# Banded attention: three more gate steps between the first scores, and VectorE scales the probabilities of the first 128 tokens

## The chip, the cores and the metric

One Trainium2 core runs the whole kernel; seven more stay unused. The metric is the device time of one execution in microseconds. The engines are TensorE (PE), VectorE (DVE), ScalarE (ACT), GpSimd (POOL) and SyncE (SP), which here only issues DMAs. Times in the traces count from the start of the profiled span.

## The reference, cut to what matters

One decoder layer over 1024 tokens of width 1024. A combined projection feeds three token mixers (a convolution, a state-space scan "SSD", banded attention) and three sigmoid gates that weigh their results; memory cross-attention and an MLP follow. The change lies in the banded attention:

```python
def swa_branch(q, k, v, q_g, k_g, sinks, rel_bias, band_dist):   # 16 heads of 64, 4 kv heads
    q, k = rms_norm(q, q_g), rms_norm(k, k_g)
    # 8 blocks of 128 queries; each sees its own 128 keys and the 128 before
    logits = einsum("bnqgrd,bnkgd->bngrqk", qb, kb) * 64 ** -0.5 + rel_bias
    logits = where(mask, logits, NEG_INF)          # 0 <= distance < 128; block 0 has no keys before it
    m = maximum(max(logits, -1), sink)
    pexp = exp(logits - m)
    probs = pexp / (sum(pexp, -1) + exp(sink - m))
    return einsum("bngrqk,bnkgd->bnqgrd", probs, vb)
...
gates = sigmoid((u @ w_in)[..., OFF_GATE:] + gate_bias)          # 24 tiles of 128 channels here
merged = gates[0] * y_a + gates[1] * y_b + gates[2] * y_c
```

## The kernel before, in words

Large products are done as three float32r products of split operands (high x high, high x low, low x high), with 128x128 weights and 512 moving columns. TensorE runs nearly without a break, and its instructions are kept in program order (`pe.on = True`). A planner orders the other engines' instructions; each engine then works its own list in order, and semaphores join them. Work under `tc.high_priority()` (weight loads and splits in `wslot`, the first splits of the merge) is planned ahead of its place in the program. Weights go through three slots: a load on SP's queue (L158), a cast on ScalarE (L162), and for the low half either a negated copy on ScalarE (L165) with an accumulating load on GpSimd's queue (L166) or a subtraction on GpSimd (L168).

The 24 gate tiles fill TensorE's time between the small, dependent matmuls of the scan and the attention. `fillers()` is a stream of steps of 3 matmuls (128x128 by 512): 21 gates of 16 steps each, then `merge_head`, 32 steps that begin the merging stage (the product of the scan's result with `w_b0`, for two output tiles at once). `fill(n)` takes `round(2 * n)` steps of that stream. A gate ends with a tanh on ScalarE (L296) and a store on SP's queue (L297). `merge_head` loads tiles of the scan's result (L308, `yin`), casts each on ScalarE (L267, `oh`) and subtracts on VectorE (L268, `ol`); its first two staging buffers are shared with the gates' tanh tiles.

The attention handles 16 pieces in `order`, eight blocks `n` of 128 tokens with two halves of 8 heads each. `scores(n, half)` is a generator with two groups: 8 matmuls of queries with keys into two PSUM banks (tile `ps_lg`), then 4 VectorE instructions (L1014) that add the bias, write the logits `lg` to SBUF and keep each row's maximum. After the second group VectorE forms the negated maximum (`nm`, L1022) and the sink's term (`es`, L1023), ScalarE the exponentials with their row sums (L1026, 8 of them), VectorE the reciprocals (`rd`, L1032), and one multiply by the reciprocals (L1033) makes probabilities of the whole piece: 128 x 8 x 128 elements in block 0, twice that in the others. `turned` transposes the probabilities on TensorE (`ps_pt`) and copies them to SBUF on ScalarE (`pT`, L1048); `values` multiplies by the values (`ps_o`) and stores the result (L1065). Small PSUM tiles share four banks (pool `pss`).

Ahead of the main loop come the scores of pieces 0 and 1 (block 0, both halves), with filler steps after each group. Pass `i` of the main loop then takes `turned` of piece `i` and `scores` of piece `i + 2` in turn, one filler step after each of the four, and `values` of piece `i - 1`. The passes 14 and 15 have no scores left. Behind the loop the rest of the fillers runs without a break (L1085).

Of the kernel before, what the change touches and what calls it, by code (L numbers as in the profile page):

```python
# [55 lines left out]
def trunk_kernel(tc, w_io):  # L56
    nc = tc.nc
    act, dve, pool = nc.scalar, nc.vector, nc.gpsimd
    ctx = ExitStack()
    with ctx:  # L60
# [29 lines left out]
        def step():  # L90

            steps_done[0] += 1
            owed[0] += pace[0]
            if owed[0] >= 1:
                owed[0] -= 1
                next(taps[0], 0)
            for i, (due, fn) in enumerate(side):
                if due <= steps_done[0]:
                    side.pop(i)
                    fn()  # L100
                    break
# [181 lines left out]
        with ExitStack() as s1:  # L283
# [43 lines left out]
            def fill(n):  # L327

                for _ in range(round(2 * n)):
                    if next(gates, 0) is None:  # L330
                        filled[0] += 1
                        if filled[0] % 2 == 0:
                            step()
# [435 lines left out]
            with ExitStack() as sc:  # L769
# [197 lines left out]
                def queries(n):  # L967
                    qn[n] = ap_.tile([P, 8, P], F32, tag="qn", name="qn", bufs=2)
                    nc.sync.dma_start(qn[n], d_q[n])
# [20 lines left out]
                def scores(n, half):  # L990

                    if half == 0 and n:
                        queries(n)
                    k0 = 0 if n else P
                    kn = 256 - k0
                    lg = at.tile([P, 8, 256], F32, tag="lg", name="lg", bufs=3)
                    mx = at.tile([P, 8], F32, tag="mx", name="mx")

                    for p2 in range(2):
                        if p2:  # L1000
                            yield
                        banks = [pss.tile([P, 512], F32, tag="s", name="ps_lg") for j in range(2)]
                        for q in range(2):
                            pr = p2 * 2 + q
                            for j in range(2):
                                kv = slice(j * 64, j * 64 + 64)
                                pe.matmul(
                                    banks[j][:, q * 256:q * 256 + kn], qn[n][kv, half * 4 + pr, :],
                                    ktp[kv, half, n * P + P - kn:n * P + P], start=True, stop=True,
                                )  # L1010
                        for q in range(2):
                            for j in range(2):
                                i = (p2 * 2 + q) * 2 + j
                                dve.tensor_tensor_reduce(  # L1014
                                    lg[:, i, k0:], banks[j][:, q * 256:q * 256 + kn], bias[:, half * 8 + i, k0:], 1.0, NEG,
                                    ALU.add, ALU.max, mx[:, i:i + 1],
                                )
                    nm = at.tile([P, 8], F32, tag="nm", name="nm")
                    es = at.tile([P, 8], F32, tag="es", name="es")
                    rs = at.tile([P, 8], F32, tag="rs", name="rs")  # L1020
                    sk = slice(half * 8, half * 8 + 8)
                    dve.scalar_tensor_tensor(nm, mx, -1.0, nsink[:, sk], ALU.mult, ALU.min)  # L1022
                    dve.tensor_sub(es, nm, nsink[:, sk])  # L1023
                    act.activation(es, es, AF.Exp)
                    for i in range(8):
                        act.activation(  # L1026
                            lg[:, i, k0:], lg[:, i, k0:], AF.Exp, bias=nm[:, i:i + 1],
                            accum_out=rs[:, i:i + 1],
                        )
                    dve.tensor_add(rs, rs, es)  # L1030
                    rd = at.tile([P, 8], F32, tag="rd", name="rd")
                    dve.reciprocal(rd, rs)  # L1032
                    pool.tensor_mul(  # L1033
                        lg[:, :, k0:], lg[:, :, k0:], rd.unsqueeze(2).to_broadcast([P, 8, kn])
                    )
                    lgs.append(lg)
                    yield
# [32 lines left out]
                lgs, pTl = [], []  # L1070
                for o in order[:2]:
                    for _ in scores(*o):
                        fill(1)
                fill(4)
                for i, o in enumerate(order):
                    pieces = [turned(*o, lgs[i]), scores(*order[i + 2]) if i + 2 < len(order) else iter(())]
                    for _ in range(2):
                        for piece in pieces:
                            next(piece, 0)
                            fill(0.5)  # L1080
                    if i:
                        values(*order[i - 1], pTl[i - 1])
# [122 lines left out]
        with ExitStack() as sc:  # L1205
# [67 lines left out]
            def attend(h, qT, outs, first, start):  # L1273
# [64 lines left out]
                for at, fn, args in (  # L1338
                    (0, scores, (0,)), (2, scores, (1,)), (5, turn, (0,)), (6, scores, (2,)), (7, turn, (1,)),
                    (8, scores, (3,)), (10, values, (0, 0)), (11, values, (0, 1)), (12, turn, (2,)), (13, turn, (3,)),  # L1340
                    (15, values, (1, 0)), (16, values, (1, 1)),
                ):
                    after(start + at, lambda fn=fn, args=args: fn(*args))
# [375 lines left out]
def build(nc, packed):  # L1719
    io = {k: nc.dram_tensor(k, v.shape, mybir.dt.from_np(v.dtype), kind="ExternalInput").ap() for k, v in packed.items()}  # L1720
    io["outT"] = nc.dram_tensor("outT", (KT, P, T), F32, kind="ExternalOutput").ap()
    with tile.TileContext(nc) as tc:
        trunk_kernel(tc, io)
# [12 lines left out]
```

## Time and profile before

| | us |
|---|---|
| median of 3 runs (range) | 2715.16 (2714.44 to 2717.03) |
| the profiled execution | 2716.95 |
| its span | 2715.2 |
| TensorE busy | 2681.2 (99%) |
| VectorE, ScalarE, GpSimd busy | 1605.4, 1074.0, 794.6 |
| attention: first and last scores start | 1184.9, 1327.9 |

Rows of the timeline give the start, the length, the engine, the line, the operation, the tiles written and read, the shapes and how many instructions are joined; the bracket holds the idle time before it and what ended it. A row of a stretch gives its length, then the busy time of each engine with its instructions, the granted TensorE clock (1.00 is full), the share of the DMA engines and the bytes moved. Matmul lengths overlap each other, so steps are read from start to start.

### The profile page before, as it was taken

Reading aid. Unit: us, or ns where it says so; the run is one execution under the profiler, and the core shown is the slowest. Engines: PE = TensorE matmul, PEld = TensorE weight load, DVE = VectorE, ACT = ScalarE, POOL = GpSimd, SP = SyncE. Lnnn points to the kernel's source line nnn. Section 1 sums busy time; section 2 is a strip of 40 time slices with the busy share of each in tenths; the row PEclk is TensorE's granted clock in tenths of the full one; section 3 lists DMA queues with packets and bytes.
Section 4 is the critical chain, followed back from the end, with each engine's and each line's share of the span. In section 5 each row is a group of like instructions: output and inputs, shape, how many; then the busy total and the mean of one; then the engine's idle time right before and its main releaser. Section 6 shows DMA issues by size and latency. Waiting matters only on the chain. (4 is left out here: it accounts for less than half of the span.)

```text
span 2715.2 us, 31722 instructions
## 1 busy us (share of the span) xinstructions
PE 2681.2 (99%) x12368; PEld 2164.6 (80%) x12368; DVE 1605.4 (59%) x1887; ACT 1074.0 (40%) x1749; POOL 794.6 (29%) x442
## 2 busy tenths in 40 slices
PE   9999999999999999999999999999998999999999
PEld 7888878888787878775588778888876888888887
DVE  7598878758666776524414773434568886532423
ACT  6533321225666656556612351324423332222221
POOL 2332221200505050414342432321115664422220
PEclk9999999999999999999999999999999999999999
DMA  7642232344555555672444332311123332454642
GB/s 249 204 131 95 96 114 88 122 125 86 148 155 148 142 146 154 179 228 76 140 178 155 117 109 93 101 58 32 59 85 109 147 132 109 179 187 140 207 134 70
DMA packets 119574, 354.79 MB, mean 131 GB/s; under 512 B 12016, under 2 KB 37120, under 8 KB 119040
## 3 DMA queue, kind: packets, MB, share of 16 engines
q1 hardware_dynamic: 112656, 328.12, 35.8%
q0 software_dynamic: 6768, 24.64, 5.4%
q8 instruction: 97, 1.59, 0.2%
q14 instruction: 53, 0.43, 0.1%
HBM read 277.06 MB, written 78.80 MB: 131 GB/s over the span
## 5 line engine op out<-in xcount | busy, mean ns | idle before, releaser
L73 PE MATMUL ps_g<-oh,wh 128*128 128x512 f32 x1872 | 604.3, 403 | 9.1 <-ACT oh L267 3.9
L73 PE MATMUL ps_g<-ol,wh 128*128 128x512 f32 x1872 | 591.8, 394 | 3.0 <-DVE ol L268 2.8
L73 PE MATMUL ps_g<-oh,wl 128*128 128x512 f32 x1872 | 582.1, 391 | 1.5 <-POOL wl L168 1.5
L168 POOL TENSOR_TENSOR wl<-ws,wh 128x1024 fp32r<-128x1024 f32 (+2 forms) x106 | 261.9, 2472 | 714.7 <-ACT wh L162 682.6
L73 PEld LDWEIGHTS ps_g<-ol,wh 128*128 128x128 f32 x1872 | 351.8, 188 | 89.3 <-issue 9.3
L73 PEld LDWEIGHTS ps_g<-oh,wl 128*128 128x128 f32 x1872 | 352.2, 188 | 77.2 <-POOL wl L168 1.9
L73 PEld LDWEIGHTS ps_g<-oh,wh 128*128 128x128 f32 x1872 | 339.0, 189 | 73.0 <-issue 5.5
L362 DVE SCALAR_TENSOR_TENSOR tapy<-hin,cst,tapy 128x1024 f32<-128x1024 f32 x240 | 354.6, 1477 | 32.7 <-ACT tapy L357 26.2
L162 ACT CAST wh<-ws 128x1024 fp32r<-128x1024 f32 (+1 forms) x169 | 176.4, 1044 | 466.9 <-PE ps_g L73 303.1
L73 PE MATMUL ps_up<-blk,st 128*128 128x512 f32 x1344 | 310.0, 393 | 8.8 <-DVE blk L1387 5.7
L73 PEld LDWEIGHTS ps_up<-blk,st 128*128 128x128 f32 x1344 | 254.3, 190 | 63.8 <-DVE blk L1387 6.3
L268 DVE TENSOR_TENSOR ol<-r_in,oh 128x1024 fp32r<-128x1024 f32 x64 | 91.7, 1437 | 222.8 <-ACT oh L267 222.8
L73 PE MATMUL ps_d<-ol,wh 128*128 128x512 f32 x512 | 199.5, 390 | 0.4 <-DVE ol L268 0.2
L73 PE MATMUL ps_d<-oh,wl 128*128 128x512 f32 x512 | 199.2, 389 | 0.0
L73 PE MATMUL ps_d<-oh,wh 128*128 128x512 f32 x512 | 199.2, 389 | 0.0
L73 PE MATMUL ps_tm<-wh,oh 128*128 128x512 f32 x448 | 175.8, 393 | 0.4 <-DVE zth L637 0.4
L73 PE MATMUL ps_tm<-wh,ol 128*128 128x512 f32 x448 | 174.6, 390 | 0.0
L73 PE MATMUL ps_tm<-wl,oh 128*128 128x512 f32 x448 | 174.4, 389 | 0.0
L166 POOL DMA_DIRECT2D wl<-w_ch x45 | 39.1, 868 | 378.6 <-ACT wl L165 378.6
L182 POOL TENSOR_TENSOR wl<-ws,wh 128x1024 fp32r<-128x1024 f32 x28 | 76.3, 2736 | 218.1 <-ACT wh L181 218.0
L267 ACT CAST oh<-r_in 128x1024 fp32r<-128x1024 f32 x64 | 67.2, 1053 | 180.1 <-PE ps_d L73 173.0
L791 DVE SCALAR_TENSOR_TENSOR c4a<-c4v,cst,c4a 128x1023 f32<-128x1023 f32 (+2 forms) x72 | 96.6, 1341 | 59.5 <-ACT c4a L789 48.4
(388 smaller groups left out, 3843.6 us busy)
## 6 DMA issues: line engine op xcount, KB each, us to landing
r_in<-d_r SPq DMA_DIRECT2D x64, 512.0 KB, 3.7
ws<-w_ch SPq DMA_DIRECT2D x63, 512.0 KB, 3.5
wl<-w_ch POOLq DMA_DIRECT2D x45, 512.0 KB, 5.8
csb<-d_cs SPq DMA_DIRECT2D x32, 512.0 KB, 4.0
gth<-d_th SPq DMA_DIRECT2D x32, 512.0 KB, 4.4
ws<-w_up SPq DMA_DIRECT2D x32, 512.0 KB, 3.3
d_r<-r SPq DMA_DIRECT2D x32, 512.0 KB, 2.6
ws<-w_down SPq DMA_DIRECT2D x32, 512.0 KB, 3.3
```

The costliest lines, as they stand in the source:

```text
L73: ins = nc.tensor.matmul(*a, **k)
L162: act.copy(wh[:, a:b], st[:, a:b])
L166: pool.dma_start(wl[:, a:b], src[:, a:b], accum_op=ALU.add)
L168: (low or pool).tensor_sub(wl[:, a:b], st[:, a:b], wh[:, a:b].bitcast(F32))
L182: pool.tensor_sub(wl[:, :, c], s3, wh[:, :, c].bitcast(F32))
L267: act.copy(a, src)
L268: dve.tensor_sub(b, src, a.bitcast(F32))
L362: dve.scalar_tensor_tensor(y, hin[:, j:j + T], w(j), y, ALU.mult, ALU.add)
L791: dve.scalar_tensor_tensor(a[:, s:], v[:, :T - s], C("c4_w", ct * 4 + 3 - s), a[:, s:], ALU.mult, ALU.add)
```

## The change

The multiply by the reciprocals is issued on VectorE for block 0 (two instructions) and on GpSimd for the other blocks as before. The steps of filler after each of the four groups of scores ahead of the main loop become 3 instead of 2; the fourth group is followed by 8 more in both versions. The number of filler steps in all is the same, so four fewer are left for the run behind the loop.

```diff
                     dve.reciprocal(rd, rs)
-                    pool.tensor_mul(
+
+                    (pool if n else dve).tensor_mul(
                         lg[:, :, k0:], lg[:, :, k0:], rd.unsqueeze(2).to_broadcast([P, 8, kn])
                     )
                     lgs.append(lg)
...
                 lgs, pTl = [], []
                 for o in order[:2]:
                     for _ in scores(*o):
-                        fill(1)
+                        fill(1.5)
                 fill(4)
                 for i, o in enumerate(order):
```

## The prediction

> **What bounds the kernel now.** I read the page first, then the chain of waits of TensorE over the attention stage (1180 to 1400 us), then the timelines of the engines there, and last the granted clock in single stretches.
>
> ```profile
> span 2715.2 us, 31722 instructions
> PE 2681.2 (99%) x12368; PEld 2164.6 (80%) x12368; DVE 1605.4 (59%) x1887; ACT 1074.0 (40%) x1749; POOL 794.6 (29%) x442
> ```
>
> TensorE is busy in 99% of the span; 34 us of idle time are all there is. An edit that moves matmuls without removing any can win or lose only in TensorE's gaps and in the clock behind them. In the stage that the diff touches these are the gaps:
>
> ```profile
> PE ps_g L73 <- ACT oh L267: 3.9, 1, 3.9
> PE ps_pt L77 <- POOL lg L1033: 2.2, 1, 2.2
> PE ps_pt L77 <- ACT pT L1048: 0.8, 2, 0.4
> PE ps_lg L73 <- DVE mx L1014: 0.8, 1, 0.8
> ```
>
> Columns: waiter, releaser, us in total, times, longest. Each has a place in the timeline of TensorE (start, length, in brackets the idle time before it):
>
> ```profile
> 1190.24 0.92 PE L73 MATMUL ps_lg<-ktp,qn 64*128 64x128 f32 x8 [0.82 <-DVE mx L1014]
> ...
> 1194.81 0.62 PE L73 MATMUL ps_g<-oh,wh 128*128 128x512 f32 x2
> ...
> 1196.17 0.62 PE L73 MATMUL ps_g<-oh,wh 128*128 128x512 f32 x2
> ...
> 1204.58 1.13 PE L73 MATMUL ps_lg<-ktp,qn 64*128 64x256 f32 x8
> ...
> 1206.45 1.03 PE L77 MATMUL ps_pt<-mat,lg 128*128 128x128 f32 x8
> ...
> 1216.03 1.97 PE L77 MATMUL ps_pt<-mat,lg 128*128 128x128 f32 x8 [2.21 <-POOL lg L1033]
> ...
> 1336.21 1.22 PE L73 MATMUL ps_g<-oh,wh 128*128 128x512 f32 x2 [3.92 <-ACT oh L267]
> ```
>
> Three places: the third group of scores (block 0, half 1) at 1190.24, the transposes of block 1, half 0 at 1216.03, and the first filler step that is no gate any more (merge head) at 1336.21. A group of 2 gate steps is 6 matmuls, 1194.81 to 1196.17, so a step is 0.68 us. A gap costs more than its length where the clock drops behind it:
>
> ```profile
> 1190.20:1193.20 3.00, 2.96 (x22) 2.30 (x22) 2.26 (x20) 1.67 (x10) 0.00 (x0) 1.00 0.91 291
> ...
> 2023.10:2025.50 2.40, 2.35 (x10) 1.99 (x11) 2.37 (x3) 0.42 (x1) 0.00 (x0) 1.00 0.54 218
> ...
> 1216.00:1219.40 3.40, 3.37 (x13) 2.63 (x15) 0.77 (x2) 3.17 (x14) 0.79 (x1) 0.50 0.90 298
> ...
> 1336.20:1341.50 5.30, 5.25 (x16) 3.95 (x17) 2.72 (x4) 4.08 (x11) 2.26 (x1) 0.50 0.84 287
> ```
>
> The third number from the end is the granted clock. After the gap of 0.82 it stayed 1.00; after 2.21 it was 0.50 for 3.4 us (1.70 us lost); after 3.92 it was 0.50 for 5.3 us (2.65 lost). So the 2.21 gap costs 3.91 and the 3.92 gap 6.57.
>
> **The change, part by part.** Fillers are issued in half-gate steps of 3 matmuls; fill(1) gives 2, fill(1.5) gives 3. The loop runs four times, so 4 more steps (12 matmuls, 4 x 0.68 = 2.7 us) stand ahead of the main loop: one after each of the four groups of scores, three of them between groups. The number of filler steps is the same, so those 2.7 us are taken from the plain run of fillers behind the loop: net nothing by themselves. What moves are places.
>
> (a) The 0.82 us wait. The third group needs the PSUM banks of the first, which VectorE frees by adding the bias; VectorE could not begin before a store had landed:
>
> ```profile
> 1189.46 0.29 DVE L1014 CUSTOM_DVE_ANT_0 lg<-ps_lg,bias 128x128 f32<-128x128 f32 x1 [32.84 <-DMA d_yb<-yt]
> ```
>
> That release is set by a DMA from before the stage and does not move. TensorE would have been ready at 1190.24 - 0.82 = 1189.42; two more steps ahead of this group bring it to 1189.42 + 1.36 = 1190.78, after the release at 1190.24. The wait goes: -0.82, no clock behind it. Late next is the fourth group, and its banks (freed by the next four reductions) come within about a microsecond, less than the 0.65 us group plus 2.0 us of steps before it.
>
> (b) VectorE's multiply for block 0 (twice 128x1024, one per half).
>
> ```profile
> 1191.28 0.17 DVE L1022 SCALAR_TENSOR_TENSOR nm<-mx,nsink 128x8 f32<-128x8 f32 x1
> ...
> 1195.80 1.81 DVE L1022 SCALAR_TENSOR_TENSOR nm<-mx,nsink 128x8 f32<-128x8 f32 x1
> 1195.69 1.89 POOL L1033 TENSOR_TENSOR lg<-lg,rd 128x1024 f32<-128x1024 f32 x1 [9.98 <-DVE mx L1014]
> 1202.68 1.89 POOL L1033 TENSOR_TENSOR lg<-lg,rd 128x1024 f32<-128x1024 f32 x1 [2.12 <-DVE rd L1032]
> L839 DVE TENSOR_TENSOR csb<-csb,cbm x32: 1211/1224/2101, 638.4 to 1142.6; 128x1024 f32<-128x1024 f32 x32
> ```
>
> The nearest VectorE row, L839, multiplies the same shape by a broadcast operand in 1.224 us against 1.89 on GpSimd. The 128x8 instruction at 1195.80 took 1.81 us and ended with GpSimd's multiply (1195.69 + 1.89 = 1197.58); undisturbed it took 0.17 (half 0, at 1191.28), so the exponentials of half 1 come up to 1.6 earlier. Queued behind VectorE's own multiply are that same small instruction and the reductions of the next scores: at most 1.22 later. Between -1.6 and +1.2 us, and neither reaches the path: half 1's probabilities were ready at 1202.68 + 1.89 = 1204.57 and transposed at 1206.45, 1.88 us later, and the 4 steps widen that. I take 0; the cover is those gate steps, and without them half 0 would be the first exposed, by at most 1.2. GpSimd still multiplies for blocks 1 to 7, so the 2.21 us wait is not addressed by this edit.
>
> (c) A gate is 16 steps and a pass of the main loop issues 4, so the end of a gate falls one pass earlier: after passes 0, 4, 8, 12 instead of 1, 5, 9, 13. With it move the cast and negated copy of the next weights and the gate's tanh on ScalarE, the weight load and the gate store on SP's queue, and the accumulating load on GpSimd's queue (in pass 5 GpSimd still sat idle 3.47 us before the multiply that followed, the last row below: nothing). What ScalarE puts ahead of the exponentials is seen where a gate ended after pass 5:
>
> ```profile
> 1251.02 1.13 PE L73 MATMUL ps_lg<-ktp,qn 64*128 64x256 f32 x8
> ...
> 1252.63 1.05 ACT L162 CAST wh<-ws 128x1024 fp32r<-128x1024 f32 x1 [1.55 <-PE ps_g L73]
> 1253.58 1.11 ACT L296 ACTIVATE gate_th<-ps_g,cst 128x1024 f32<-128x1024 f32 x1
> 1254.59 1.05 ACT L165 ACTIVATE wl<-wh 128x1024 fp32r<-128x1024 f32 x1
> 1255.54 0.19 ACT L1024 ACTIVATE es<-es 128x8 f32<-128x8 f32 x1
> ...
> 1260.29 3.59 POOL L1033 TENSOR_TENSOR lg<-lg,rd 128x2048 f32<-128x2048 f32 x1 [3.47 <-ACT pT L1048]
> ```
>
> From the second group of scores to the end of GpSimd's multiply: 1260.29 + 3.59 - 1251.02 = 12.86 us. For block 1, half 0, with no gate end in it, it is
>
> ```profile
> 1212.37 3.60 POOL L1033 TENSOR_TENSOR lg<-lg,rd 128x2048 f32<-128x2048 f32 x1 [7.80 <-PE ps_g L73]
> ```
>
> 1212.37 + 3.60 - 1204.58 = 11.39. After the change a gate ends just there (after pass 0), so I take 12.86 - 11.39 = +1.47 on the wait of 2.21, which becomes 3.7. Bounds: 0, if ScalarE keeps the exponentials first; and 1.47 + (2.65 - 1.70) = 2.42, if the longer gap halves the clock for as long as after 3.92. I take 1.47, since in passes 1, 5 and 9 alike the three copies came first.
>
> (d) The gates run out after pass 12, so the merge head starts in pass 13 instead of 14. Its first step waits for ScalarE's casts, which stand behind five exponentials:
>
> ```profile
> 1323.11 0.46 SPq L308 DMA_DIRECT2D yin<-d_yb  x1
> DMA to landing us min/median/max: 3.4/5.1/7.4
> ...
> 1332.56 0.21 ACT L1024 ACTIVATE es<-es 128x8 f32<-128x8 f32 x1 [1.54 <-DVE es L1023]
> ...
> 1335.13 1.98 ACT L267 CAST oh<-yin 128x1024 fp32r<-128x1024 f32 x2
> ```
>
> All that sets this (last gate's tanh, freed staging buffer, load, casts, the weights' subtraction on GpSimd) moves along by one pass, so I keep its 6.57 us; its cost is 0 of difference, bounded by -6.57 (the casts go first). But in the old order this gap also hid another lateness, that of the last probabilities (block 7, half 1):
>
> ```profile
> 1327.36 1.13 PE L73 MATMUL ps_lg<-ktp,qn 64*128 64x256 f32 x8
> ...
> 1331.19 1.09 PE L77 MATMUL ps_pt<-mat,lg 128*128 128x128 f32 x8
> ...
> 1344.99 1.09 PE L77 MATMUL ps_pt<-mat,lg 128*128 128x128 f32 x8
> ...
> 1349.66 3.65 PE L73 MATMUL ps_o<-pT,vt 128*64 128x512 f32 x16
> ...
> 1339.24 3.60 POOL L1033 TENSOR_TENSOR lg<-lg,rd 128x2048 f32<-128x2048 f32 x1 [6.79 <-DVE rd L1032]
> ```
>
> Their chain took 1339.24 + 3.60 - 1327.36 = 15.48 us, and TensorE reached them only at 1344.99 because it had been held up. Undisturbed, TensorE gets there in 1331.19 - 1327.36 = 3.83, plus pass 14, which has no scores left and costs 1349.66 - 1344.99 = 4.67 and half of the 3.65 for its values, 1.83: 10.33 us. With the merge head's gap one pass earlier, it no longer covers this. The new wait is the chain less 10.33: 11.39 gives 1.06, 12.86 gives 2.53, 15.48 gives 5.15. Some casts and subtractions of the merge head still mix with the chain, but no gate end does, so I take the middle row: 2.53 us, and behind it the half clock that the nearest gap (2.21) drew, 1.70 us; together +4.23. Bounds +1.06 (short gap, full clock) and 5.15 + 2.65 = +7.80.
>
> Here a rule can be weighed against the trace. The row after 2.21 us of idle shows the clock at 0.50; the row at 2023 follows a gap of 2.63 us and shows 1.00, so the length alone does not decide. The Trainium skill, "TensorE: Matmul & The Clock Gate", Part 1, lets the clock fall after an idle window of about 3.4 us, the window running freely. By that rule a gap of 2.53 would cost no clock, and the forecast would be 1.70 lower, 2718.3. The trace differs at 1216 and agrees at 2023; I go by the row of this stage.
>
> **Sum.** -0.82 (a) + 0 (b) + 1.47 (c) + 4.23 (d) = +4.88 us. The profiled execution took 2716.95 us, 1.75 more than its span and 1.79 more than the median, 2715.16; the sum on the execution is 2721.8, and on the median 2720.0. My own range for this case: -0.82 + 0 + 1.06 = +0.2 to -0.82 + 2.42 + 7.80 = +9.4, so 2715.4 to 2724.6. About 0.2%, 5.4 us, is what a measurement of this kernel can tell from no change; the forecast lies just inside it.
>
> **Rivals.**
> 1. Slower: in (d) the exponentials of block 7, half 1 stand behind casts whose loads have not landed, so that its chain takes 15.48 again with nothing to cover it: -0.82 + 1.47 + 7.80 = +8.45, 2723.6. It ends beyond 0.2% once that wait with its clock exceeds 4.8 us. For: 15.48 is the measured length of exactly this chain. Against: part of it came from the gate end and from GpSimd's subtraction, which both move away. 0.15.
> 2. Hidden anyway: block 7 is on time, because the merge head's operands and exponentials are interleaved in another way. -0.82 + 1.47 = +0.65, 2715.8. For: only 1.06 us are missing with the shortest chain. 0.15.
> 3. The change does only what its first line says: as 2, and ScalarE puts the exponentials ahead after pass 0. -0.82, 2714.3. Against: the order in passes 1, 5 and 9. 0.08.
> 4. Faster: the casts of the merge head go ahead of the exponentials in pass 13, and its gap goes: -0.82 + 1.47 - 6.57 = -5.92, 2709.2. For: by the median of the loads their input has landed at 1323.11 + 5.1 = 1328.2, 7 us before the cast. Against: the casts' readiness moves along with the gate's end, so their order need not change. 0.12.
>
> The forecast has 0.50; about 0.17 of it lies above 2720.6. Slower: 0.17 + 0.15 = 0.32. Faster: rival 4 less its half-microsecond margin, 0.10. The rest 0.58. The range reaches to rival 4 and to the top of my own: 2709 to 2725.
>
> **What would show it.** (a) right: the third scores start without a bracket. (b) right: two VectorE multiplies of about 1.2 us in L1034's place, the 128x8 instruction of block 0, half 1 at about 0.2, no TensorE wait on either. (c) right: TensorE waits about 3.7 us for GpSimd at block 1, with cast, tanh and copy ahead of its exponentials; wrong if that wait stays at 2.2 or is gone. (d) right: a gap on the merge head's casts in the pass that still holds the last scores, and a second one on GpSimd's multiply two passes later. The prediction fails if the order in which ScalarE takes casts and exponentials changes, or if gaps elsewhere, in the merging stage above all, come or go.

## The result, and the profile after

The changed kernel is slower: 2727.76 us median of 6 runs (2724.62 to 2729.59) against 2716.38 for the kernel before in the same series (2714.44 to 2718.87). The ratio is 1.0039, 95% interval 1.0029 to 1.0049. (The ratios here and below are estimates with an interval, not the quotients of the two medians beside them, from which they differ by up to 0.0006.) One execution of the kernel with the phase alone was slow (3363.86 us) and is left out of its ratio, but not of its median in the table below, which would be 2728.41 without it. The profiled execution took 2726.24 us, 9.3 more than that of before. The forecast was 2720.0 with a range of 2709 to 2725: the sign that it leaned to is right, the size was too small, and the range ends below the measurement. Slower by more than 0.2% had been given 0.32.

The row of the engines on the page stands nearly as before; TensorE's waits in the attention stage (1180 to 1400 us), below it, do not:

```profile
PE 2684.7 (99%) x12368; PEld 2168.2 (80%) x12368; DVE 1606.3 (59%) x1889; ACT 1075.4 (39%) x1749; POOL 789.0 (29%) x440
```

```profile
PE ps_pt L77 <- POOL lg L1034: 10.3, 2, 6.4
PE ps_g L73 <- ACT oh L267: 3.9, 1, 3.9
PE ps_pt L77 <- ACT pT L1049: 1.6, 3, 0.7
PE ps_g L73 <- DVE ol L268: 0.2, 1, 0.2
```

TensorE has the same 12368 matmuls. Its wait for GpSimd's multiply grew from 2.2 us in one place to 10.3 in two; the wait for the third scores is gone. The timeline of TensorE gives the places:

```profile
1185.50 0.71 PE L73 MATMUL ps_lg<-ktp,qn 64*128 64x128 f32 x8
...
1191.33 0.82 PE L73 MATMUL ps_lg<-ktp,qn 64*128 64x128 f32 x8
...
1207.00 1.14 PE L73 MATMUL ps_lg<-ktp,qn 64*128 64x256 f32 x8
...
1220.18 1.97 PE L77 MATMUL ps_pt<-mat,lg 128*128 128x128 f32 x8 [3.91 <-POOL lg L1034]
...
1331.54 1.07 PE L73 MATMUL ps_g<-oh,wh 128*128 128x512 f32 x2 [3.93 <-ACT oh L267]
...
1337.85 1.14 PE L73 MATMUL ps_lg<-ktp,qn 64*128 64x256 f32 x8
...
1343.23 0.66 PE L77 MATMUL ps_pt<-mat,lg 128*128 128x128 f32 x4 [0.73 <-ACT pT L1049]
...
1355.79 1.97 PE L77 MATMUL ps_pt<-mat,lg 128*128 128x128 f32 x8 [6.39 <-POOL lg L1034]
...
1379.44 0.73 PE L73 MATMUL ps_g<-oh,wh 128*128 128x512 f32 x2
```

Block 1, half 0 waits 3.91 us at 1220.18. The merge head waits 3.93 at 1331.54, now ahead of the last scores (1337.85). The last piece, block 7 half 1, waits 6.39 at 1355.79, where before there was no wait at all. The first and the last of these rows bound the stage; the rows of before that answer to them are

```profile
1184.89 0.71 PE L73 MATMUL ps_lg<-ktp,qn 64*128 64x128 f32 x8
...
1369.82 0.73 PE L73 MATMUL ps_g<-oh,wh 128*128 128x512 f32 x2
```

From the first scores to the first product behind the merge head is the same work in both kernels: 1369.82 - 1184.89 = 184.93 us before, 1379.44 - 1185.50 = 193.94 after. The stage lost 9.01 of the 9.3 us. The granted clock behind the gaps (third number from the end):

```profile
1220.10:1223.40 3.30, 3.22 (x13) 2.47 (x13) 0.72 (x3) 3.22 (x14) 0.03 (x1) 0.50 0.26 79
1223.40:1226.00 2.60, 2.60 (x11) 1.69 (x11) 0.70 (x5) 1.87 (x6) 0.00 (x0) 0.51 0.00 0
1331.50:1335.40 3.90, 3.67 (x12) 1.84 (x12) 2.73 (x4) 3.37 (x9) 0.83 (x1) 0.56 0.79 269
1355.70:1359.20 3.50, 3.41 (x13) 3.08 (x14) 0.00 (x0) 1.17 (x2) 0.04 (x1) 0.52 0.00 0
```

With the clock's share the places cost: block 1, 3.91 + 5.9 x 0.50 = 6.86 us (3.91 before); merge head, 3.93 + 0.19 (its next product, on VectorE's `ol`) + 3.9 x 0.44 = 5.84 (6.57 before); the last piece, 0.73 (the transposes of block 7, half 0, which wait for a copy of `pT` on ScalarE) + 6.39 + 3.5 x 0.48 = 8.80 (nothing before); third scores, 0 (0.82 before). Together 21.5 against 11.3, +10.2, for 9.01 measured: the clock's part is read from windows, and 1.2 us of it is not accounted for.

### The profile page after: what moved, and what is told of

It reads as the page before. It is cut to its first block, busy times and chain, and to the rows that moved or that the text cites. A ratio compares the mean times of both kernels' runs of the same rounds, so it can differ in the third digit from the quotient of the medians.

```text
span 2724.5 us, 31710 instructions
## 1 busy us (share of the span) xinstructions
PE 2684.7 (99%) x12368; PEld 2168.2 (80%) x12368; DVE 1606.3 (59%) x1889; ACT 1075.4 (39%) x1749; POOL 789.0 (29%) x440
```

## Experiments: is it the place where gates end, or something else?

My theory after the result: the loss comes from the four steps alone, and only through the pass in which gates and then the merge head begin (their phase). Rivals: VectorE's multiply delays something; or the steps between the first scores do harm where they stand.

**Four runs that take the change apart.** The first (e1) keeps the steps and gives block 0's multiply back to GpSimd; the second (e2) keeps the multiply and takes the steps out; the third (e3) keeps both, and takes four steps out behind the fourth group, so that 16 stand ahead of the main loop as in the kernel before; the fourth (e4) has neither part, but four more steps behind the fourth group, so that only the phase moves.

```diff
# first, against after
-                    (pool if n else dve).tensor_mul(
+                    pool.tensor_mul(
# second, against after
-                        fill(1.5)
+                        fill(1)
# third, against after
-                fill(4)
+                fill(2)
# fourth, against before
-                fill(4)
+                fill(6)
```

> The added steps alone; GpSimd multiplies in every block. Phase theory (the added steps move every gate's end, and with it the start of the merge head, one pass earlier; all of the loss follows from that): as slow as the changed kernel, 9 to 12 us over the kernel before (2725 to 2729), with TensorE waits of about 3.9 us on GpSimd at block 1 and about 6.4 us on GpSimd at the last piece. Multiply theory (VectorE's multiplies lengthen its queue and reorder the stage): within 2 us of before.

> VectorE's multiply for block 0 alone; 2 steps after each of the first scores as before. Phase theory: within 2 us of before (2714 to 2718), the waits of 0.82, 2.2 and 3.9 us of the kernel before still there. Multiply theory: 9 to 12 us slower.

> Both edits kept, but the run of 8 steps behind the first scores is cut to 4, so that 16 steps stand ahead of the loop as before and every gate ends where it ended before. Phase theory: the wait of 0.82 us is gone, the others are those of the kernel before, time 1 us under before at most 2 over (2714 to 2718). Rival (steps between the first scores hurt by themselves, by making the first chains late): still 6 us or more over before.

> The kernel before with 4 more steps in the run behind the first scores (8 becomes 12) and nothing else: the gates end a pass earlier, the steps between the first scores stay 2, GpSimd multiplies everywhere. Phase theory: 9 to 13 us slower than before, the wait of 0.8 us at the third scores still there, about 3.9 us at block 1 and 6.4 us at the last piece. Rival (the steps between the scores do it): within 2 us of before.

| | median us | before us | ratio, 95% |
|---|---|---|---|
| e1, steps alone | 2728.51 | 2717.05 | 1.0043 (1.0030 to 1.0057) |
| e2, multiply alone | 2719.12 | 2717.05 | 1.0005 (0.9997 to 1.0014) |
| e3, both, phase kept | 2715.21 | 2717.05 | 0.9991 (0.9982 to 1.0000) |
| e4, phase alone | 2729.06 | 2717.05 | 1.0044 (1.0030 to 1.0057) |

TensorE's waits in the same stretch, of the steps alone, and then of the kernel with both edits and the phase kept:

```profile
PE ps_pt L77 <- POOL lg L1034: 10.0, 2, 6.2
PE ps_g L73 <- ACT oh L267: 3.9, 1, 3.9
PE ps_lg L73 <- DVE mx L1014: 1.8, 1, 1.8
```

```profile
PE ps_g L73 <- ACT oh L267: 3.9, 1, 3.9
PE ps_pt L77 <- POOL lg L1034: 2.5, 1, 2.5
...
PE ps_lg L73 <- DVE mx L1014: 0.3, 1, 0.3
```

Steps alone and phase alone lose as much as the whole change; the phase alone has the same places, 9.9 us for GpSimd's multiply in two and 3.9 at the merge head. The multiply alone loses nothing that can be measured, though its median lies 2.07 us over before, just beyond what was expected. With both edits and the old phase there is one wait on GpSimd again, of 2.5 us, and no loss. So neither the multiply nor the place of the steps between the scores does harm; the phase does, and that is shown from both sides. The last kernel is the lowest median of these five, but its interval ends at 1.0000: it is not shown to be faster than before.

**What makes the last piece late (e5).** In the changed kernel the splits of the merge head's eight operand tiles (a cast on ScalarE and a subtraction on VectorE for each) are all planned ahead. This run plans the first two ahead and emits each of the others two tiles before it is needed.

```diff
-                for k in range(KT):
-                    with tc.high_priority():
-                        y = staging[k % 2].tile([P, T], F32, tag="glu", name="yin")
-                        nc.sync.dma_start(y, d_yb[k])
-                        parts.append(split(opa if k < 4 else opb, y))
+                def part(k):
+                    y = staging[k % 2].tile([P, T], F32, tag="glu", name="yin")
+                    nc.sync.dma_start(y, d_yb[k])
+                    parts.append(split(opa if k < 4 else opb, y))
+                with tc.high_priority():
+                    part(0)
+                    part(1)
...
                 for k in range(KT):
+                    if k + 2 < KT:
+                        part(k + 2)
```

> The changed kernel, with only the first two of the merge head's eight casts and subtractions planned ahead of their place; the other six follow one by one with its steps, so that six casts instead of eight stand ahead of the last piece's exponentials, and none that still waits for its load. If the last piece (block 7, half 1) is late because ScalarE and VectorE first serve casts and subtractions of the merge head: TensorE's wait for GpSimd there falls from 6.4 us to between 0 and 2.5 and the time by 5 to 8 us (2720 to 2723). If it is late because pass 14 is short and the chain long, whatever stands ahead: the wait stays at 4 us or more and the time within 3 us of the changed kernel's.

2720.68 us against 2717.44: 1.0010 (1.0001 to 1.0019). The excess over before, each in its own series, fell from 11.4 us to 3.2. TensorE's timeline and the clock at the last piece, and ScalarE's first exponential of it:

```profile
1353.68 1.09 PE L77 MATMUL ps_pt<-mat,lg 128*128 128x128 f32 x8 [1.85 <-POOL lg L1040]
```

```profile
1353.70:1357.00 3.30, 3.30 (x23) 2.99 (x24) 2.14 (x2) 1.39 (x3) 0.00 (x0) 1.00 0.52 144
```

```profile
1340.20 1.05 ACT L267 CAST oh<-yin 128x1024 fp32r<-128x1024 f32 x1
...
1341.63 2.95 ACT L267 CAST oh<-yin 128x1024 fp32r<-128x1024 f32 x3
...
1345.22 0.51 ACT L1032 ACTIVATE lg<-lg,nm 128x256 f32<-128x256 f32 x1 [0.64 <-DVE nm L1028]
```

The wait went from 6.39 to 1.85 us and lost its half clock, with four casts ahead of the exponentials instead of six and no wait for a load between them, and with one subtraction ahead of the last reductions instead of four. That is 8.80 - 1.85 = 6.95 us by the trace, and the first of the two cases that were set out. The edit moves casts and subtractions together, so it does not part their shares. Block 1's 3.91 and the merge head's 3.93 are unchanged, as they should be. From the first scores to the first product behind the merge head this profiled execution took 1375.82 - 1186.14 = 189.68 us, 4.26 less than the changed kernel's; 1.11 of it is a wait for the third scores, which the changed kernel did not have, and the clock behind the merge head's gap stayed at 0.50 for 6.4 us, where the changed kernel showed 0.56 for 3.9.

**Both late places mended (j1).** The same, and VectorE also multiplies for block 1:

```diff
-                    (pool if n else dve).tensor_mul(
+                    (pool if n > 1 else dve).tensor_mul(
```

> The changed kernel with both of its new waits treated: the late splits of e5, and VectorE instead of GpSimd multiplies in block 1 as well (2 x 1.2 us instead of 3.6, and no GpSimd multiply for the small VectorE instructions to stand behind). If the loss is the chain of block 1 with a gate's end in it and the chain of the last piece behind the merge head's casts, and nothing else: the wait at block 1 falls from 3.9 to about 2.7, the last one to about 1.9 as in e5, 1 to 3 us under e5 and within 2 us of before (2716 to 2720). If something else carries part of the loss: no less than e5 (2720.7) or more.

2719.32 us against 2716.40: 1.0006 (0.9998 to 1.0015), not to be told from no change, though the median lies 2.9 us over before, where 2 at most was expected. The multiply moved to VectorE shortens block 1's wait to 2.67 us at full clock:

```profile
1220.20 1.06 PE L77 MATMUL ps_pt<-mat,lg 128*128 128x128 f32 x8 [2.67 <-DVE nm L1028]
```

```profile
1220.20:1223.40 3.20, 3.20 (x21) 2.37 (x22) 0.95 (x3) 3.20 (x14) 0.00 (x0) 1.00 0.26 82
```

From the first scores to the first product behind the merge head this profiled execution took 1371.89 - 1186.93 = 184.96 us, against 184.93 before and 193.94 in the changed kernel. The two places account for the loss: with them mended the earlier phase costs nothing that is measured, and by the interval 0.15% (4 us) at most. It gains nothing either. What block 1's mending is worth is less sure than the last piece's: the ratios without and with it, 1.0010 and 1.0006, lie within each other's intervals, and it was not run by itself.

**Looking for a kernel that beats both.** The phase that harms when moved earlier might help when moved later, or block 1 be given more time. Six tries (g1, g2, f1, h1, i1 and i2 in this order); an edit is shown against the changed kernel or, where its comment names another try, against that:

```diff
# later phase: 12 steps ahead of the main loop
-                        fill(1.5)
-                fill(4)
+                        fill(1)
+                fill(2)
# later phase with steps of 1.5: 12 steps ahead
-                fill(4)
+                fill(0)
# hold block 1: as later phase, and the four steps put ahead of block 1's transposes
+                    if i == 2:
+                        fill(2)
# hold and later: as hold block 1, and four single steps left out in passes 4, 6, 9, 11
-                    for _ in range(2):
+                    for rnd in range(2):
...
-                            fill(0.5)
+                            fill(0 if rnd and i in (4, 6, 9, 11) and piece is pieces[0] else 0.5)
# later phase, and VectorE multiplies for block 1
-                    (pool if n else dve).tensor_mul(
+                    (pool if n > 1 else dve).tensor_mul(
# that, and two steps moved from behind the first scores to ahead of them
-                fill(3)
+                fill(4)
-                fill(2)
+                fill(1)
```

> VectorE's multiply for block 0, 2 steps after each of the first scores and 4 behind them: 12 steps ahead of the loop instead of 16, so the gates end one pass later than in the kernel before (after passes 2, 6, 10, 14) and the merge head starts in pass 15, with no exponentials left to stand ahead of its casts. Phase theory: the gap at the merge head falls from 3.9 us to about 1, the last piece waits about 1 us, 4 us under before (2711 to 2714), the wait at block 1 stays about 2.2. Rival (a pass of shift either way costs, since 16 steps fit best): 2719 or more.

> Both edits of the change kept, and the run of 8 steps behind the first scores left out: 12 steps ahead of the loop, 3 after each group, so that the merge head starts in pass 15 as in g1 and the third scores wait as little as in e3. If the two gains add up: 2 to 5 us under before (2711 to 2714.5). Rival: with nothing behind the first scores, block 0's transposes come before its probabilities are scaled and wait 1 to 3 us, so that the gain is given back (2716 or more).

> VectorE's multiply for block 0, 2 steps after each of the first scores, 4 instead of 8 steps behind them, and the 4 that are saved put at the end of pass 1, ahead of block 1's transposes: 16 steps by then as before, so every later gate ends where it ended in the kernel before. If TensorE's wait of 2.2 us at block 1 is only a lack of cover: it is gone with its half clock, 3.9 us under before (2712 to 2714). Rival (the chain of block 1 slides along, or block 0's transposes now come too early): no gain, 2716 or more.

> The steps held back to the end of pass 1 as in f1, and one step fewer in each of passes 4, 6, 9 and 11, so that the gates run out one pass later as in g1. If both gains stand by themselves: 8 us under before (2707 to 2711), with neither the gap at block 1 nor that of 3.9 us at the merge head. Rival (the passes with a step fewer begin to wait for their probabilities): 2713 or more.

> As g1 (12 steps ahead of the loop, gates and merge head one pass later than in the kernel before), and VectorE multiplies in block 1 too. Expected: TensorE's wait at block 1 falls from 2.5 us to about 1.3, 1 to 2 us under g1 (2712 to 2715). Rival: VectorE, now holding the 2.4 us multiply, is late with the biases of the next scores and the gain is given back (2716 or more).

> As i1, and two of the four steps behind the first scores moved ahead of them, so that the third group of scores comes 1.4 us later and no longer waits for the store that holds VectorE back (0.3 to 3.9 us in the runs so far, by when that store lands). Expected: 1 to 2 us under i1 in the median and a smaller spread, 3 to 6 us under before (2711 to 2714). Rival: that store lands later when TensorE's scores do, so the wait stays; then as i1.

| | median us | before us | ratio, 95% |
|---|---|---|---|
| g1, later phase | 2715.74 | 2717.44 | 1.0000 (0.9991 to 1.0008) |
| g2, later phase, steps of 1.5 | 2716.86 | 2718.28 | 0.9995 (0.9986 to 1.0004) |
| f1, hold block 1 | 2717.73 | 2717.44 | 1.0003 (0.9994 to 1.0012) |
| h1, hold and later | 2719.64 | 2717.44 | 1.0005 (0.9996 to 1.0013) |
| i1, later phase, block 1 on VectorE | 2715.88 | 2716.40 | 1.0001 (0.9992 to 1.0010) |
| i2, that, two steps ahead | 2717.89 | 2716.40 | 1.0006 (0.9997 to 1.0015) |

None differs from the kernel before by what can be measured, and all six medians lie above the range in which a gain had been expected. The traces show other waits in place of those shortened, 1.26 us at block 0's transposes with steps of 1.5 and 2.15 us there in the last try. Hold block 1 shows it best. Its four steps should have covered block 1's wait; the timelines of TensorE, GpSimd, VectorE and ScalarE:

```profile
1222.69 1.97 PE L77 MATMUL ps_pt<-mat,lg 128*128 128x128 f32 x8 [3.10 <-DVE mx L1014]
```

```profile
1211.92 3.60 POOL L1034 TENSOR_TENSOR lg<-lg,rd 128x2048 f32<-128x2048 f32 x1 [11.09 <-ACT pT L1049]
```

```profile
1213.06 2.48 DVE L1022 SCALAR_TENSOR_TENSOR nm<-mx,nsink 128x8 f32<-128x8 f32 x1
...
1221.71 0.17 DVE L1030 TENSOR_TENSOR rs<-rs,es 128x8 f32<-128x8 f32 x1 [2.55 <-ACT lg L1026]
```

```profile
1218.22 1.03 ACT L162 CAST wh<-ws 128x1024 fp32r<-128x1024 f32 x1
...
1219.65 1.04 ACT L165 ACTIVATE wl<-wh 128x1024 fp32r<-128x1024 f32 x1
```

Half 0's probabilities are in time, and TensorE waits 3.10 us for something else: `nm` of half 1 stood 2.48 us until GpSimd's multiply ended (2.40 in the kernel before), a cast and a copy of a gate's end then came between its exponentials, and the sum `rs`, which waits for them on VectorE, stands there ahead of the reductions that free the PSUM banks. In the later phase the merge head's wait fell from 3.93 to 1.73 us and the last piece's to 0.98, but block 1 kept 2.48 and the third scores 1.30.

## Why the prediction was wrong, by its own steps

**(a) was right here, but its release is not fixed.** The third scores start without a wait, -0.82 as forecast. "That release is set by a DMA from before the stage and does not move" was too strong: with the steps alone, which are the same steps, TensorE still waited:

```profile
1192.59 1.27 PE L73 MATMUL ps_lg<-ktp,qn 64*128 64x128 f32 x8 [1.75 <-DVE mx L1014]
```

The store's landing moves by some microseconds against the first scores from run to run; over the profiles here this wait lay between 0 and 3.9 us. A term of 0.82 there is within that scatter; that it came out is luck.

**(b) was right.** VectorE's rows of block 0 in the changed kernel, and `nm` of block 1 half 1 further on:

```profile
1197.28 1.22 DVE L1034 TENSOR_TENSOR lg<-lg,rd 128x1024 f32<-128x1024 f32 x1
...
1199.16 0.17 DVE L1022 SCALAR_TENSOR_TENSOR nm<-mx,nsink 128x8 f32<-128x8 f32 x1
...
1203.12 1.22 DVE L1034 TENSOR_TENSOR lg<-lg,rd 128x1024 f32<-128x1024 f32 x1
...
1216.63 3.52 DVE L1022 SCALAR_TENSOR_TENSOR nm<-mx,nsink 128x8 f32<-128x8 f32 x1
```

Twice 1.22 us, `nm` of half 1 down from 1.81 to 0.17, and no wait of TensorE on either; alone the multiply is 1.0005 (0.9997 to 1.0014).

**(c) was right in kind; its clock was sized too small.** ScalarE works off the gate's end ahead of block 1's exponentials, as passes 1, 5 and 9 had shown:

```profile
1208.60 1.05 ACT L162 CAST wh<-ws 128x1024 fp32r<-128x1024 f32 x1 [4.21 <-PE ps_g L73]
1209.55 1.11 ACT L296 ACTIVATE gate_th<-ps_g,cst 128x1024 f32<-128x1024 f32 x1
1210.56 1.05 ACT L165 ACTIVATE wl<-wh 128x1024 fp32r<-128x1024 f32 x1
```

```profile
1216.53 3.60 POOL L1034 TENSOR_TENSOR lg<-lg,rd 128x2048 f32<-128x2048 f32 x1 [3.77 <-DVE rd L1032]
...
1352.14 3.60 POOL L1034 TENSOR_TENSOR lg<-lg,rd 128x2048 f32<-128x2048 f32 x1 [13.96 <-DVE rd L1032]
```

The chain took 1216.53 + 3.60 - 1207.00 = 13.13 us (12.86 taken), the wait 3.91 (3.7). The clock stayed halved for 5.9 us instead of 3.4, so the term is 6.86 - 3.91 = +2.95 and not +1.47; the upper bound given, 2.42, was passed too.

**(d) is the step that failed.** The merge head's own cost carried over (5.84 for 6.57), and the last piece did lose its cover, the time for which TensorE had been held up elsewhere. The sum gave it 2.53 + 1.70 = 4.23 us, and it measured 8.80. The formula, chain less 10.33, held: the last row above ends the chain at 1352.14 + 3.60, the second scores of the piece began at 1337.85, which is 17.89 us and leaves 7.56; the two waits measured 0.73 + 6.39 = 7.12. What failed is the length put into it: "Some casts and subtractions of the merge head still mix with the chain, but no gate end does, so I take the middle row", 12.86. ScalarE and VectorE of the changed kernel show what mixed in:

```profile
1337.36 3.89 ACT L267 CAST oh<-yin 128x1024 fp32r<-128x1024 f32 x4
...
1343.16 1.05 ACT L267 CAST oh<-yin 128x1024 fp32r<-128x1024 f32 x1
...
1345.91 1.05 ACT L267 CAST oh<-yin 128x1024 fp32r<-128x1024 f32 x1 [1.22 <-DMA yin<-d_yb]
...
1347.34 0.51 ACT L1026 ACTIVATE lg<-lg,nm 128x256 f32<-128x256 f32 x1
```

```profile
1338.44 4.63 DVE L268 TENSOR_TENSOR ol<-yin,oh 128x1024 fp32r<-128x1024 f32 x4 [1.50 <-ACT oh L267]
1342.99 0.42 DVE L1014 CUSTOM_DVE_ANT_0 lg<-ps_lg,bias 128x256 f32<-128x256 f32 x1
...
1345.50 0.16 DVE L1022 SCALAR_TENSOR_TENSOR nm<-mx,nsink 128x8 f32<-128x8 f32 x1
```

Four subtractions (4.63 us) stand ahead of the last reductions, which start at 1342.99 with their scores long done (1337.85 + 1.14), and a fifth ahead of `nm`, which ends at 1345.66. The exponentials could start there and start at 1347.34, behind a sixth cast that itself waited 1.22 us for its load. The chain of 15.48 from which I took my upper end had only two of these casts in it (1335.13, 1.98 us, quoted there); in the old order the other six came behind the last exponentials. That is near rival 1, casts with unlanded loads ahead of the exponentials, given 0.15, and it went beyond the 8.45 it was priced at. But the load makes 1.22 us at most of the 17.89 - 11.39 = 6.50 that the chain has over the one without a gate's end. VectorE makes more: its reductions start 1342.99 - 1337.85 = 5.14 us behind their scores, against 1205.75 - 1204.58 = 1.17 in block 1, half 0 of the kernel before, and the fifth subtraction takes another 1.22. The prediction had mentioned the subtractions and put no price on them. What I had and did not use: these splits are planned ahead of their place, and with the merge head one pass earlier the last piece's scores come after the first two casts, so that all six remaining ones can stand ahead of its exponentials.

The sum with the measured terms is -0.82 + 2.95 - 0.73 + 8.80 = +10.2; the forecast's was +4.88. Of the difference of 5.3 us the last piece makes 4.6 and the clock at block 1 1.5; the merge head gives 0.7 back.

## What to carry to other kernels

Filler work that is moved between small dependent steps also moves everything that hangs on its end; before adding steps, look up in which pass the fillers now run out and what the wait there was covering. When a wait moves off something that it covered, count which instructions will stand ahead of the uncovered chain in each engine's order, read-ahead ones with their loads too, and don't take the length of the chain from a pass in which they stood elsewhere. In a stage as full as this one a shortened wait can hand its time to the next one: here none of six tries gained.

## What the runs showed of the hardware

The length of a gap did not decide the clock behind it. The kernel with the later phase, at block 1, and the changed kernel in the merging stage each had a gap of 2.48 us; here each gap with the clock behind it:

```profile
1214.65 1.09 PE L77 MATMUL ps_pt<-mat,lg 128*128 128x128 f32 x8 [2.48 <-POOL lg L1034]
```

```profile
1214.60:1218.00 3.40, 3.35 (x21) 2.49 (x22) 1.25 (x6) 3.28 (x14) 0.00 (x0) 1.00 0.25 80
```

```profile
2031.95 1.19 PE L73 MATMUL ps_g<-oh,wh 128*128 128x512 f32 x2 [2.48 <-DVE ht L1351]
```

```profile
2031.90:2034.00 2.10, 2.05 (x5) 1.70 (x6) 2.06 (x3) 0.12 (x1) 0.00 (x0) 0.50 0.62 250
```

Full behind the first, half behind the second, where the kernel before had kept full clock after 2.63. Nor did the place decide it: at the same product of the merging stage the kernel with both edits and the old phase waited 2.48 us too and kept a clock of 1.00 (2021.60 to 2023.70). The Trainium skill, "TensorE: Matmul & The Clock Gate", Part 1, has a free-running window of about 3.4 us, after which, if it was idle, the clock halves. That the lot differs from place to place and from run to run agrees with a window that runs freely; that it halves behind 2.48 us does not agree with a whole window of idle, and there the measurement decides. What separates the two cases is not settled here.

The VectorE instruction `nm` of 128x8, started while GpSimd multiplies, lasts until that ends: 3.52 us at 1216.63 (GpSimd's row at 1216.53 ends at 1220.13) and 2.48 in hold block 1, against 0.17 alone. The Trainium skill, "SBUF — State Buffer", section "SBUF: two separate sides", says that a VectorE instruction with two SBUF inputs and a GpSimd one that reads SBUF exclude each other for the whole instruction; the trace agrees. Not expected was that the wait of so small an instruction would be part of TensorE's next wait once the steps were moved.
